# A bench of constant matmuls ahead of the first conditioning product

## The chip, the core and the metric

The kernel runs on one core of a Trainium2 chip. The metric is the device time of one execution in microseconds (us); the lower, the better. Engines are named as in the profile: PE is TensorE's matmul, PEld its weight load, DVE is VectorE, ACT is ScalarE, POOL is GpSimd and SP is SyncE, which here only issues transfers.

## What is computed

One decoder layer is applied to 256 prompt tokens and 32 sample tokens (8 sequences of 4), 288 tokens in all, of width 2048:

```python
def _layer(x, c, conv_prefix, chunk, ...):
    mod = (silu(c) @ w_ada + b_ada).reshape(n, 6, 1, 2048)      # conditioning
    sh_m, sc_m, gt_m, sh_f, sc_f, gt_f = [mod[:, i] for i in range(6)]
    h = _rms(x, g_mix) * (1 + sc_m) + sh_m
    b_gate, c_gate, hc, u, v, ga, gb = split(h @ w_in)          # 2048 -> 9216
    ya = b_gate * short_conv(c_gate * hc)
    yb = gelu(u) * spatial_gate(_rms(gelu(v), g_v))
    merged = sigmoid(ga) * (ya @ w_pa) + sigmoid(gb) * (yb @ w_pb)
    x = x + gt_m * (merged @ w_out)
    h2 = _rms(x, g_ffn) * (1 + sc_f) + sh_f
    gate, up = split(h2 @ w_ffn_in)                             # 2048 -> 2 x 5632
    x = x + gt_f * ((silu(gate) * up) @ w_ffn_out)
```

A last normalisation follows. Returned are the tokens, the new convolution state and the normalised v rows, all in float32.

## The kernel before

Tokens lie along the free dimension and features along the 128 partitions, so a product of 128 output features is a chain of matmuls, each 128x128 weights against 128x288 activations. Every float32 operand is split into a high and a low part in float32r, and one step of a product is three matmuls (`triple`, L221 to L231): high weights with high activations, high weights with low activations, low weights with high activations. These are lines L224, L227 and L229 of the profile, and nearly all of the kernel.

Weights come from memory in blocks of up to 128x2048 into seven rotating buffers named `raw`; ScalarE casts the high part (L448) and VectorE subtracts to get the low part (L454). Activation parts, intermediate results and small tables live in 92 rotating buffers named `s`, of 1,192 bytes per partition each. In the built program a slot begins 32, 96, 160 or 224 bytes past a multiple of 256, and a weight part 96 bytes past one.

The conditioning product `silu(c) @ w_ada` is cut into nine units (a0, a1, aC, aD, aE, a2 to a5) and done by `Ada.run` (L388). The first unit, a0, is the first real work of TensorE. Ahead of it, and in gaps between the first steps, stand matmuls on a bfloat16 tile of ones, `wb`, whose result goes to a PSUM tile `idle` and is read by nobody:

```python
    def warm(n, out=None):
        out = idle if out is None else out
        for _ in range(n):
            PE.matmul(out[:, :T], wb[:, :P], wb, start=True, stop=True)
    ...
    steps = [Do(lambda: warm(24)), a0[0], Do(lambda: warm(5)), a0[1]]
```

TensorE's order is that in which the code is written. The orders of ScalarE, VectorE and SyncE are also the written ones from the first load on, until the head of the kernel is over. A load into a `raw` buffer waits until the tile that had the buffer before has been read for the last time, and all loads are issued from SyncE, one behind the other.

The head goes: load of the two blocks of a0, of the first weights (w0) and the first tile of x, of the two blocks of a1, of the second tile of x, of wK and of the first wA; meanwhile 24 matmuls on ones, a0, the first tile of the activations, the product w0 with it, a1, the second tile, the product wK, and then the stream of weight blocks.

Of the kernel before, what the change touches and what calls it, by code (L numbers as in the profile page):

```python
# [8 lines left out]
F32 = mybir.dt.float32  # L9
F32R = mybir.dt.float32r  # L10
# [4 lines left out]
P = 128  # L15
D = 2048
T = 288
TP = 256
TU = T + 10
# [5 lines left out]
RAW = 7  # L25
# [59 lines left out]
def decoder_kernel(tc, d):  # L85
    nc = tc.nc
    from contextlib import ExitStack

    with ExitStack() as es:
        def pool(name, bufs=1, **kw):  # L90
            return es.enter_context(tc.tile_pool(name=name, bufs=bufs, **kw))

        pc = pool("const")
        pw = pool("wstream")
        pslot = pool("slots", SLOTS)
        ptmp = pool("tmp", 5)
        pps = pool("psum", 4, space=bass.MemoryType.PSUM)
        with tc.manual_schedule(engines={nc.tensor.engine}):
            _body(tc, nc, d, pc, pw, pslot, ptmp, pps)


def _body(tc, nc, d, pc, pw, pslot, ptmp, pps):
    ids = [0]

    def nm(s):
        ids[0] += 1
        return f"{s}_{ids[0]}"

    def const(name, shape, dt=F32):
        return pc.tile(shape, dt, tag=name, name=name)  # L110

    def slot(dt=F32, shape=(P, T)):
        return pslot.tile(list(shape), dt, tag="s", name=nm("s"), padded_shape=[P, TU])
# [4 lines left out]
    def psmain():  # L118
        return pps.tile([P, 512], F32, tag="main", name=nm("pm"), bufs=4)
# [4 lines left out]
    V, A, G, PE, SY = nc.vector, nc.scalar, nc.gpsimd, nc.tensor, nc.sync  # L124
# [227 lines left out]
    class Step:  # L352
        defer = False
        raw = None
# [209 lines left out]
    wb = const("wb", [P, 288], BF16)  # L564
    G.memset(wb, 1.0)
    idle = psmain()
# [475 lines left out]
        tail.close()  # L1042


    rh1 = h1.__getitem__
    def at(main, plan):
        out, n = [], 0
        for s in main:
            out.append(s)
            if isinstance(s, Blk):  # L1050
                n += 1
                out += plan.pop(n, [])
        assert not plan
        return out
# [70 lines left out]
    n = len(steps)  # L1125
    stream = [s for s in steps if not isinstance(s, Do)]
    pos = {id(s): i for i, s in enumerate(stream)}
    order = list(stream)
# [27 lines left out]
    for s in steps:  # L1156
# [11 lines left out]
        i = pos[id(s)]  # L1168
# [124 lines left out]
```

## Time and profile before

| | |
|---|---|
| median of the runs | 1625.04 us (1625.02 to 1625.06, 2 runs) |
| profiled execution, its own time | 1625.02 us |
| its span, first to last instruction | 1623.2 us |
| TensorE matmul, busy | 1613.2 us, 12645 instructions |
| TensorE weight load, busy | 1549.3 us |
| VectorE / ScalarE, busy | 1015.8 / 736.2 us |
| DMA | 357.6 MB, mean 220 GB/s |
| granted TensorE clock | 0.998 |

In a row of groups the columns are line, engine, operation, out<-in by the program's names, shape, number of instructions, then busy time in us and mean ns of one, then the idle time of the engine just before them and what ended it. Matmuls are pipelined: one lasts some 0.29 us from its start to its modelled end while the next has long started, so how fast TensorE works is read from the starts, or from the number of matmuls in a stretch of time.

### The profile page before, as it was taken

The numbers are of one execution on the slowest core, as the hardware profiler recorded it, in microseconds if no ns is written. First come the engines' busy times: TensorE is split into PE (matmuls) and PEld (weight loads), VectorE is DVE, ScalarE is ACT, GpSimd is POOL, SyncE is SP. The second block draws the span as 40 slices with busy tenths as digits, with TensorE's granted clock in tenths as the row PEclk, the third lists the DMA queues.
The fourth block names the chain that finished last, engine by engine and source line by source line (L and its number), as shares of the span: only waits on it lengthen the run. The fifth ranks groups of instructions, "written<-read, shape, count | busy, mean of one in ns | idle before, by whom it ended". The sixth has DMA issues, their size and how long they took to land.

```text
span 1623.2 us, 31599 instructions
## 1 busy us (share of the span) xinstructions
PE 1613.2 (99%) x12645; PEld 1549.3 (95%) x12645; DVE 1015.8 (63%) x2196; ACT 736.2 (45%) x1358; POOL 21.8 (1%) x66
## 2 busy tenths in 40 slices
PE   9999999999999999999999999999999999999997
PEld 8998999999999999999999999999999999999997
DVE  6676788877755567667744555555555555555565
ACT  5533344643444334456633444444444444444454
POOL 0000000000000000011000000000000000000000
PEclk9999999999999999999999999999999999999999
DMA  9887866777877666654576556453464434645341
GB/s 376 324 318 286 313 238 212 273 284 289 298 292 309 261 260 228 241 178 158 185 307 263 207 180 209 156 173 110 164 229 157 168 121 161 225 157 172 110 161 59
DMA packets 59140, 357.60 MB, mean 220 GB/s; under 512 B 6736, under 2 KB 9840, under 8 KB 28272
## 3 DMA queue, kind: packets, MB, share of 16 engines
q1 hardware_dynamic: 58704, 355.45, 60.0%
q8 instruction: 99, 1.62, 0.4%
q14 instruction: 49, 0.40, 0.1%
q10 hardware_dynamic: 288, 0.13, 0.0%
HBM read 352.46 MB, written 3.09 MB: 219 GB/s over the span
## 4 chain that ended last, share of the span: by engine, by line
PE 98%; DMA 1%; DVE 0%; DVEq 0%; ACT 0%; issue 0%; ACTq 0%
PE pm L224 31%; PE pm L227 31%; PE pm L229 30%; PE ada L388 5%; DMA raw<-in_wK 1%; DMA raw<-in_w 0%; DVE st L1023 0%; DMA ct<-in_c 0%; PE px L227 0%; PE px L818 0%; PE px L224 0%; PE px L229 0%; PE px L859 0%; PE px L198 0%; PE px L860 0%; PE px L861 0%
## 5 line engine op out<-in xcount | busy, mean ns | idle before, releaser
L224 PE MATMUL pm<-s,hi 128*128 128x288 f32 (+1 forms) x3750 | 1108.9, 296 | 0.0
L227 PE MATMUL pm<-s,hi 128*128 128x288 f32 (+1 forms) x3750 | 1105.0, 295 | 0.0
L229 PE MATMUL pm<-s,lo 128*128 128x288 f32 (+1 forms) x3738 | 1101.3, 295 | 0.0
L448 ACT CAST hi<-raw 128x512 fp32r<-128x512 f32 (+1 forms) x963 | 587.4, 612 | 812.0 <-PE pm L227 776.7
L454 DVE TENSOR_TENSOR lo<-raw,hi 128x512 fp32r<-128x512 f32 (+1 forms) x849 | 577.2, 681 | 439.2 <-ACT hi L448 426.8
L224 PEld LDWEIGHTS pm<-s,hi 128*128 128x128 f32 x3750 | 705.1, 188 | 15.2 <-issue 13.3
L227 PEld LDWEIGHTS pm<-s,hi 128*128 128x128 f32 x3750 | 704.7, 188 | 0.0
L229 PEld LDWEIGHTS pm<-s,lo 128*128 128x128 f32 x3738 | 702.7, 188 | 0.0
L243 DVE TENSOR_TENSOR lo<-raw,hi 128x512 fp32r<-128x512 f32 x111 | 74.7, 676 | 29.6 <-ACT hi L448 28.9
L388 PE MATMUL ada<-raw,cs 128*32 128x512 f32 (+2 forms) x1152 | 88.3, 452 | 0.0
L388 PEld LDWEIGHTS ada<-raw,cs 128*32 128x32 f32 x1152 | 30.9, 110 | 44.7 <-issue 42.0
L766 DVE TENSOR_TENSOR s<-pm,s 128x288 f32<-128x288 f32 x72 | 32.9, 457 | 19.8 <-PE pm L229 19.8
L298 DVE TENSOR_TENSOR s<-t,s 128x288 fp32r<-128x288 f32 (+1 forms) x76 | 34.6, 459 | 6.4 <-ACT s L296 6.4
L296 ACT CAST s<-t 128x288 fp32r<-128x288 f32 (+1 forms) x76 | 32.5, 433 | 12.9 <-DVE t L798 12.4
L338 DVE SCALAR_TENSOR_TENSOR x<-pm,mod,x 128x256 f32<-128x256 f32 x79 | 37.5, 475 | 0.0
L944 DVE SCALAR_TENSOR_TENSOR t<-t,pm 128x288 f32<-128x288 f32 x42 | 19.1, 454 | 20.6 <-PE pm L229 20.6
L758 DVE TENSOR_TENSOR s<-pm,s 128x288 f32<-128x288 f32 x48 | 21.8, 454 | 10.4 <-PE pm L229 9.5
L337 DVE TENSOR_TENSOR t<-pm,mod 128x32 f32<-128x32 f32 x79 | 15.2, 192 | 18.5 <-PE pm L229 18.5
L743 DVE SCALAR_TENSOR_TENSOR s<-pm,s 128x256 f32<-128x256 f32 x48 | 23.1, 480 | 4.1 <-PE pm L229 4.1
L749 DVE TENSOR_TENSOR s<-s,rb 128x288 f32<-128x288 f32 x48 | 21.5, 449 | 0.0
L172 ACT ACTIVATE t<-x 128x288 f32<-128x288 f32 x29 | 12.9, 445 | 17.4 <-DVE x L341 17.4
L177 DVE TENSOR_TENSOR acc<-acc,t 128x288 f32<-128x288 f32 x33 | 15.0, 456 | 8.2 <-ACT t L172 8.2
(158 smaller groups left out, 479.7 us busy)
## 6 DMA issues: line engine op xcount, KB each, us to landing
raw<-in_fi SPq DMA_DIRECT2D x84, 1024.0 KB, 4.9
raw<-in_a SPq DMA_DIRECT2D x64, 1024.0 KB, 8.8
raw<-in_f SPq DMA_DIRECT2D x64, 704.0 KB, 4.0
raw<-in_wD SPq DMA_DIRECT2D x34, 1024.0 KB, 5.7
raw<-in_aE SPq DMA_DIRECT2D x16, 1024.0 KB, 10.3
raw<-in_wo SPq DMA_DIRECT2D x16, 1024.0 KB, 6.4
raw<-in_wC SPq DMA_DIRECT2D x19, 768.0 KB, 5.7
raw<-in_pa SPq DMA_DIRECT2D x8, 1024.0 KB, 5.9
```

What stands on the lines that cost most here:

```text
L224: PE.matmul(out, wh, ah, start=first, stop=False)
L227: end_ = PE.matmul(out, wh, al, start=False, stop=turn and last)
L229: end_ = PE.matmul(out, wl, ah, start=False, stop=last)
L243: lows.pop(0)[1]()
L296: A.copy(hi, a)
L298: V.tensor_tensor(lo, a, hi.bitcast(F32), ALU.subtract)
L338: V.scalar_tensor_tensor(x[:, m, :TP], ps[:, :TP], mod[:, gt0 + m, 0:1], x[:, m, :TP], ALU.mult, ALU.add)
L388: PE.matmul(acc[32 * j : 32 * j + 32, :w], cs[:, kt, :], self.raw[:, o : o + w], start=kt == 0, stop=kt == 15, tile_position=(0, 32 * j), ...
L448: A.copy(hi, self.raw[:, s * 128 : e * 128])
L454: sub()
L743: V.scalar_tensor_tensor(t[:, :TP], ps[:, :TP], t[:, T : T + 1], t[:, :TP], ALU.add, ALU.add)
L766: V.tensor_tensor(a, ps[:, :T], a, ALU.add)
```

## The change

A function `bench` is added and called once, before the steps of the program are put together, so its instructions stand ahead of all other work in each engine's written order. It takes four `raw` buffers and 64 `s` buffers, fills one with the constant 0.75, copies that into three float32r tiles (r0, r1, r2) and into the 64 slots, and has TensorE multiply them into `idle`: first 48 matmuls on `wb`; then weights from r0 and activations from r2, both shifted by 1 to 4 elements, the activations in 64 places; then pairs of weights and activations in the main product's order of three at chosen places; then the same order with activations from slots and weights shifted by 0 to 15 elements. No result is read. The outputs and the rest of the program are the same, apart from the buffers that it gets.

```diff
+    def bench():
+        import random
+
+        f = pw.tile([P, 2048], F32, tag="raw", name=nm("bench"), bufs=RAW)
+        V.memset(f, 0.75)
+        rs = []
+        for i in range(3):
+            r = pw.tile([P, 2048], F32R, tag="raw", name=nm("benchr"), bufs=RAW)
+            A.copy(r, f) if i else V.tensor_copy(r, f)
+            rs.append(r)
+        r0, r1, r2 = rs
+        ms = []
+        for i in range(64):
+            m = slot(F32R, (P, TU))
+            (A.copy if i % 2 else V.tensor_copy)(m, f[:, :TU])
+            ms.append(m)
+
+        def mm(s, m):
+            PE.matmul(idle[:, :T], s, m, start=True, stop=True)
+
+        def w(r, k, s=0):
+            return r[:, P * (k % 12) + s : P * (k % 12) + s + P]
+
+        def mv(r, o):
+            return r[:, o : o + T]
+
+        for i in range(48):
+            mm(wb[:, :P], wb)
+        for s in (1, 2, 3, 4):
+            for o in range(64):
+                for i in range(14):
+                    mm(w(r0, i, s), mv(r2, o + s))
+        rng = random.Random(1)
+        for a in [12 + 16 * i for i in range(16)] + [144, 48, 240, 0]:
+            for b in rng.sample(range(64), 16):
+                for i in range(6):
+                    mm(w(r0, i), mv(r2, a // 4))
+                    mm(w(r0, i), mv(r2, 512 + a // 4))
+                    mm(w(r1, i, b), mv(r2, a // 4))
+        order = "212030111323010323020333020010212333202030202131"
+
+        def mixed(sh, sl, n):
+            for i in range(16):
+                h, l = (ms[(4 * i + 2 * j + int(order[3 * i + j]) % n) % 64 // 4 * 4 + int(order[3 * i + j]) % n * (4 // n)][:, :T] for j in (0, 1))
+                mm(w(r0, i, sh), h)
+                mm(w(r0, i, sh), l)
+                mm(w(r1, i, sl), h)
+
+        for s in range(16):
+            mixed(s, s, 2)
+        for sh in range(16):
+            for sl in range(16):
+                mixed(sh, sl, 4)
+
+    bench()
```

TensorE's queue at the start of the program, before. The first matmuls are those on ones, the next the first conditioning block (`ada` is its PSUM tile, `raw` its weights, `cs` the conditioning vectors):

```order
L1278 UNCONDITIONAL_BRANCH [waits barrier_Pool_Activation_PE_DVE_SP_release]
L571 LDWEIGHTS wb [waits Pool_49]
L571 MATMUL pm_96<-wb 128x288
...
L388 MATMUL ada_164<-raw_99,cs 32x64 [waits DMAHW1_49,DVE_49]
L388 MATMUL ada_164<-raw_99,cs 32x64 x15
```

The same place in the changed program. `benchr_99`, `benchr_101` and `benchr_103` are r0, r1 and r2, a name with `s` is one of the 64 slots, `pm_96` is `idle`:

```order
L1333 UNCONDITIONAL_BRANCH [waits barrier_Pool_Activation_PE_DVE_SP_release]
L1063 LDWEIGHTS wb [waits Pool_49]
L1063 MATMUL pm_96<-wb 128x288
...
L1063 MATMUL pm_96<-benchr_103,benchr_99 128x288 [waits DVE_49,Activation_49]
L1063 MATMUL pm_96<-benchr_103,benchr_99 128x288 x3585
L1063 MATMUL pm_96<-benchr_103,benchr_101 128x288
...
L1063 MATMUL pm_96<-s_105,benchr_99 128x288 [waits DVE_49]
...
L571 LDWEIGHTS wb
L571 MATMUL pm_96<-wb 128x288
...
L388 MATMUL ada_22748<-raw_22683,cs 32x64 [waits DMAHW2_49]
```

The whole bench has come between the program's start and the first matmuls on ones of before; it waits for the constants at its first float32r matmul and at the slots, and for nothing else.

SyncE's queue from the third conditioning block on, before (a `DMAHW` semaphore counts earlier transfers):

```order
L370 DMA raw_111<-in_a 128x1024 [waits DMAHW3_49]
L370 DMA raw_111<-in_a 128x1024 [waits DMAHW4_49]
L370 DMA raw_114<-in_a 128x1024 [waits DMAHW5_49]
L370 DMA raw_114<-in_a 128x1024 [waits DMAHW6_49]
L146 DMA x<-in_x 128x288 [waits DMAHW7_49]
L432 DMA raw_118<-in_wK 128x768 [waits DMAHW0_49]
L432 DMA raw_120<-in_wA 128x1024 [waits DMAHW1_49]
```

And in the changed program, where the third block gets the buffer of the constant fill, the fourth that of r0, wK that of r1 and wA that of r2:

```order
L370 DMA raw_22695<-in_a 128x1024 [waits DMAHW3_49,DVE_49,Activation_49]
L370 DMA raw_22695<-in_a 128x1024 [waits DMAHW4_49]
L370 DMA raw_22698<-in_a 128x1024 [waits DMAHW5_49,PE_49]
L370 DMA raw_22698<-in_a 128x1024 [waits DMAHW6_49]
L146 DMA x<-in_x 128x288 [waits DMAHW7_49]
L432 DMA raw_22702<-in_wK 128x768 [waits DMAHW0_49,PE_49]
L432 DMA raw_22704<-in_wA 128x1024 [waits DMAHW1_49,PE_49]
```

The order of the loads is the same; three of them now wait for TensorE, the third conditioning block for the copies on VectorE and ScalarE.

## The prediction

> **What bounds the kernel now.** I read the page first: its span, the busy shares, the granted clock and the chain that ended last.
>
> ```profile
> span 1623.2 us, 31599 instructions
> PE 1613.2 (99%) x12645; PEld 1549.3 (95%) x12645; DVE 1015.8 (63%) x2196; ACT 736.2 (45%) x1358; POOL 21.8 (1%) x66
> PEclk9999999999999999999999999999999999999999
> PE 98%; DMA 1%; DVE 0%; DVEq 0%; ACT 0%; issue 0%; ACTq 0%
> ```
>
> TensorE is busy for 99% of the span, the clock is granted throughout, and 98% of the chain that set the end is TensorE's own work. There is no idle time in which added TensorE work could disappear: what is put into its queue moves the end by what it takes. So the whole question is how fast TensorE goes through it.
>
> The duration of a matmul does not tell that, since matmuls overlap. The pace, from one start to the next, does. I took it from the stage table, in three stretches that hold little beside the main product (columns: the stretch, its length, then busy time and number of instructions of each engine, granted clock, DMA share, GB/s).
>
> ```profile
> core 0: us, PE busy (x) PEld busy (x) DVE busy (x) ACT busy (x) POOL busy (x), PEclk, DMA share, GB/s
> 900.00:1200.00 300.00, 300.00 (x2271) 300.00 (x2270) 166.03 (x328) 128.45 (x224) 0.00 (x0) 1.00 0.51 171
> 1200.00:1500.00 300.00, 300.00 (x2273) 300.00 (x2272) 163.18 (x300) 131.44 (x229) 0.00 (x0) 1.00 0.49 167
> 1500.00:1600.00 100.00, 100.00 (x758) 100.00 (x757) 60.25 (x129) 53.21 (x99) 0.00 (x0) 1.00 0.34 116
> ```
>
> 300 us over 2273 matmuls is 0.1320 us; over 2271 it is 0.1321 us, and 100 over 758 is 0.1319 us. The pace of the 128x288 product with float32r operands is therefore 0.132 us, and it stays there while the DMA share falls from 0.51 to 0.34, so transfers into the memory that TensorE reads do not set it. A look at single instructions shows the same steps of 0.13 and 0.14 us with no idle time between:
>
> ```profile
> 1250.25 0.29 PE L224 MATMUL pm<-s,hi 128*128 128x288 f32 x1
> 1250.39 0.29 PE L227 MATMUL pm<-s,hi 128*128 128x288 f32 x1
> 1250.52 0.30 PE L229 MATMUL pm<-s,lo 128*128 128x288 f32 x1
> 1250.65 0.29 PE L224 MATMUL pm<-s,hi 128*128 128x288 f32 x1
> ```
>
> Last I read the start of the program in order of time, because the change stands there.
>
> ```profile
> 1.12 5.24 PE L571 MATMUL pm<-wb 128*128 128x288 bf16 x24 [1.12 <-POOL wb L565]
> 4.83 0.32 ACT L155 ACTIVATE ctt<-ct 128x144 f32<-128x144 f32 x1 [1.90 <-DMA ct<-in_c]
> 6.29 1.10 PE L388 MATMUL ada<-raw,cs 128*32 128x64 f32 x64
> 7.32 0.79 PE L571 MATMUL pm<-wb 128*128 128x288 bf16 x5
> 9.43 0.62 ACT L448 CAST hi<-raw 128x512 fp32r<-128x512 f32 x1 [4.27 <-DMA raw<-in_w]
> 10.05 1.15 PE L571 MATMUL pm<-wb 128*128 128x288 bf16 x8
> 11.36 0.82 PE L501 MATMUL pm<-s,hi 128*128 128x298 f32 x4 [0.15 <-ACT s L677]
> 12.02 0.71 PE L503 MATMUL pm<-s,lo 128*128 128x298 f32 x4
> 17.87 1.21 PE L388 MATMUL ada<-raw,cs 128*32 128x64 f32 x64
> ```
>
> The first conditioning product is the row at 6.29. Ahead of it stand 24 matmuls on constants in bfloat16. A row of several merged matmuls lasts from the first start to the last end, so two rows of one kind give the pace: (1.15 - 0.79) / 3 = 0.12 us for bfloat16 later on. The 24 went slower: the end of the last lies about 0.79 - 4 x 0.12 = 0.31 us behind its start, so (5.24 - 0.31) / 23 = 0.214 us each.
>
> **The change part by part.** It removes and reorders nothing. It adds 22,448 matmuls, all 128x288, to the head of TensorE's queue: 48 on the bfloat16 constant, then 4 x 64 x 14 = 3584, then 20 x 16 x 6 x 3 = 5760, then 16 x 16 x 3 = 768 and 256 x 16 x 3 = 12288 on float32r constants. The last four make 22,400.
>
> *The 48 in bfloat16.* TensorE still starts at 1.12. The first 24 take 5.24 us as before, the other 24 take 24 x 0.12 = 2.9 us: they end at 9.24.
>
> *Making the constants.* One VectorE fill, one VectorE and two ScalarE copies of 2048 columns stand before the first float32r matmul. ScalarE reaches its two copies behind the activation that ends at 4.83 + 0.32 = 5.15. The cast of 512 columns took 0.62 us, so four of them bound one copy from above at 2.48 us, and both end by 10.1 at the latest. If the cost of a copy is partly fixed, they end before 9.24. I take 9.24, with 0 to 0.9 us of wait. The 64 small copies that follow are first read after 3584 + 5760 matmuls, over a millisecond later, which hides them.
>
> *The 22,400 in float32r.* Same shape, types and order as the main product, each with its own weights, no accumulation, one output bank. At 0.132 us they take 2956.8 us. What the trace does not show is a start address of weights or activations off the main product's places, so this price needs ends. Below, it is the pace of the bfloat16 constants, 0.12 us: 2688 us. Above, it is a pace at which a weight load no longer hides behind the matmul before it. The weight loads have this row:
>
> ```profile
> L224 PEld LDWEIGHTS pm<-s,hi 128*128 128x128 f32 x3750 | 705.1, 188 | 15.2 <-issue 13.3
> L224 PE MATMUL pm<-s,hi 128*128 128x288 f32 (+1 forms) x3750 | 1108.9, 296 | 0.0
> ```
>
> One load lasts 188 ns, so that end is 22,400 x 0.188 = 4211 us. I take 0.132, the row that is nearest: it has the same operation, shape and types, and in it the activation tiles already start at four different places in 256 bytes against one place of the weights, with no difference between stages. That no result is accumulated changes little: the four first matmuls at 11.36, which do not accumulate, start 12.02 - 11.36 = 0.66 us ahead of the next group, 0.165 us each with a slow first, and the accumulating four at 12.02 go at (0.71 - 0.30) / 3 = 0.137 us for 298 columns.
>
> The Trainium skill, "TensorE: Matmul & The Clock Gate", section "Back-to-back issue gap", gives the warm gap as N / 2.4 + 2.5 ns, which is 122.5 ns at 288 columns. The bfloat16 rows agree with it (0.12 us) and the float32r stages don't (0.132 us); by it the 22,400 would be estimated at 2744 us.
>
> *What stands behind them.* Everything from the row at 1.12 on now starts when the last of them has started. From there the old program has 1623.2 - 1.12 = 1622.1 us. Its 24 constants now run at the later pace: 1.15 + 16 x 0.12 = 3.07 instead of 5.24 us, 2.2 us less. The head's transfers are the other part. Of the seven load buffers the change occupies four; the first two conditioning blocks, the first weights and the third conditioning block land long before TensorE asks for them. The fourth conditioning block waits on SyncE until TensorE has read the constants for the last time, and behind it on that queue wait the second tile of x, the next weights (wK) and all later loads. Before, the critical chain had this load:
>
> ```profile
> 10.53 9.19 DMA raw<-in_wK
> ```
>
> 9.19 us is the longest landing of the head. The fourth block is asked for at 17.87, which is 17.87 - 1.12 - 2.2 = 14.6 us behind the release, so it is covered by about 5 us, and fewer transfers compete. Were that cover gone, the excess, a few us, would be paid once. wK is issued right behind it, earlier against its use than the 10.53 - 1.12 - 2.2 = 7.2 us of before. So the queue costs nothing, and TensorE's gaps in the head can at most close:
>
> ```profile
> 10.00:20.00 10.00, 9.85 (x189) 8.67 (x180) 6.64 (x21) 4.26 (x12) 0.10 (x1) 1.00 1.04 405
> 20.00:30.00 10.00, 9.66 (x69) 9.34 (x68) 7.60 (x18) 8.82 (x19) 0.00 (x0) 1.00 1.02 406
> ```
>
> That is 0.15 + 0.34 us; I count 0.2. The rest takes 1622.1 - 2.4 = 1619.7 us. The tiles of the main product move to other buffers, which by the three stages (0.1319 to 0.1321) is worth 12,000 x 0.0002 = 2.4 us either way.
>
> *The sum.* 9.24 + 2956.8 + 1619.7 = 4585.7 us of span. The profiled execution took 1625.02 us for a span of 1623.2, 1.8 more, and the median of the two runs is 1625.04, the same. The forecast is 4585.7 + 1.8 = 4587.5, rounded to 4588 us.
>
> **The rivals.** *The added product goes at the bfloat16 pace.* The main product may lose 0.012 us per matmul to a conflict between reading weights and reading activations that depends on their places; places that avoid it would give 0.12 us and 9.24 + 2688 + 1619.7 + 1.8 = 4319 us. For it speaks that single steps of 0.13 and 0.14 alternate. Against it: the change goes through nearly all places, so it would have to help at most of them. A time under 4460, a mean pace under 0.1263, gets 0.07. The gap formula named above is this case.
>
> *Odd places make weight loads or reads slow.* At the upper end it gives 9.24 + 4211 + 1619.7 + 1.8 = 5842 us, and if half the matmuls are hit (5842 + 4588) / 2 = 5215 us. No row shows a start that is not a multiple of 32 bytes, so nothing speaks against it directly; but the load has room, since a pace of 0.132 is kept with loads of 188 ns that overlap. Over 4720, a mean pace over 0.138, gets 0.09. Constants that leave the clock at its early pace (0.214 us, some 6430 us) are within it at 0.01; the bfloat16 constants did reach 0.12.
>
> *Not slower: matmuls whose result nobody reads do not run.* Then 48 + 22,400 would fall away and the time would be 1625 us or less by the 2.2 us. It decides once fewer than (32.5 - 5.7) / 0.132 = 203 of the 22,400 run, 32.5 us being 2% (about what a measurement of this kernel can tell from no change) and 5.7 us the net cost of the 48. Against it: the constants of L571 are read by nobody either, and the trace has them. The built order has every added matmul. 0.015.
>
> **How the numbers follow.** The likeliest case, a mean pace within 0.1263 to 0.138, has 0.825 and gives 4588 us. The range is its own, 4460 to 4720: the lower end lies halfway from 0.132 to 0.12, the upper just past the 0.137 us that the wider 298-column product shows at 12.02 (22,400 x 0.137 + 1630.7 = 4700). It leaves out 0.07 below, 0.09 above and 0.015 far below. All cases but the last are slower by over 2%: slower 0.985, same 0.01, faster 0.005.
>
> **What would show it.** Right: a group of 22,400 matmuls ahead of the conditioning product, no idle time in it, a stage table with 2270 or so matmuls in each 300 us, the granted clock at 1.00, and the row that was at 6.29 at about 2969 us, with the end about 1617 us behind it. Also right: DMA nearly still from about 25 us to 2966. Wrong: stages inside the added product whose paces differ by more than 5%, which would make the place of an operand a price of its own; idle time before its first float32r matmul beyond 1 us; a wait on the fourth conditioning block or on wK behind it.

## The result, and the profile after

The changed kernel takes 4598.29 us (median of 2 runs, 4598.27 to 4598.31) against 1625.04 us, a ratio of 2.8296 with a 95% interval of 2.8175 to 2.8418. The forecast was 4588 us with a range of 4460 to 4720.

The page of the changed kernel, its top and two of its groups:

```profile
span 4596.5 us, 76567 instructions
PE 4586.0 (100%) x35093; PEld 4521.1 (98%) x35093; DVE 1026.7 (22%) x2230; ACT 750.3 (16%) x1392; POOL 21.3 (0%) x66
PEclk9999999999999999999999999999999999999999
PE 100%; DVE 0%; ACT 0%; DMA 0%; issue 0%; DVEq 0%
L1063 PE MATMUL pm<-s,benchr 128*128 128x288 f32 x13056 | 1732.4, 295 | 0.0
L1063 PE MATMUL pm<-benchr,benchr 128*128 128x288 f32 x9344 | 1234.3, 294 | 0.2 <-ACT benchr L1053 0.2
```

All 9344 + 13056 = 22,400 matmuls ran, with 0.2 us of idle time ahead of them and none between. TensorE is busy throughout and the clock is granted. The stage table of TensorE, in stretches of the bench's four float32r parts (500 to 800 and 1000 to 1230 lie in the second, 1240 to 1345 is nearly all of the third, the last two lie in the fourth):

```profile
core 0: us, PE busy (x), PEclk, DMA share, GB/s
9.30:300.00 290.70, 290.70 (x2183) 1.00 0.02 7
500.00:800.00 300.00, 300.00 (x2287) 1.00 0.00 1
1000.00:1230.00 230.00, 230.00 (x1751) 1.00 0.00 1
1240.00:1345.00 105.00, 105.00 (x793) 1.00 0.04 12
2000.00:2300.00 300.00, 300.00 (x2264) 1.00 0.00 1
2600.00:2900.00 300.00, 300.00 (x2264) 1.00 0.00 1
```

The paces are 290.7 / 2183 = 0.1332 us, 0.1312, 0.1314, 0.1324, 0.1325 and 0.1325. They are within some 1.5% of each other and of the main product's 0.1320 before. A stretch also counts the two or three matmuls that reach into it from before its start, so paces read in this way are 0.1 to 0.3% low. The two ends of the bench, and what follows it, in order of time:

```profile
1.12 7.55 PE L1063 MATMUL pm<-wb 128*128 128x288 bf16 x48 [1.12 <-POOL wb L565]
8.86 21.40 PE L1063 MATMUL pm<-benchr,benchr 128*128 128x288 f32 x159 [0.20 <-ACT benchr L1053]
2975.27 3.11 PE L571 MATMUL pm<-wb 128*128 128x288 bf16 x24
2978.31 1.10 PE L388 MATMUL ada<-raw,cs 128*32 128x64 f32 x64
2983.38 0.68 PE L501 MATMUL pm<-s,hi 128*128 128x298 f32 x3 [0.15 <-ACT s L677]
2984.69 0.30 PE L501 MATMUL pm<-s,hi 128*128 128x298 f32 x1 [0.63 <-issue]
```

The float32r part lasts from 8.86 to 2975.27, 2966.4 us, and the rest of the program from there to 4596.5, 1621.2 us.

### The profile page after: what moved, and what is told of

Read it like the earlier page. It is cut to its first block, busy times and chain, and to the rows that moved or that the text cites. A ratio compares the mean times of both kernels' runs of the same rounds, so it can differ in the third digit from the quotient of the medians.

```text
span 4596.5 us, 76567 instructions
## 1 busy us (share of the span) xinstructions
PE 4586.0 (100%) x35093; PEld 4521.1 (98%) x35093; DVE 1026.7 (22%) x2230; ACT 750.3 (16%) x1392; POOL 21.3 (0%) x66
## 4 chain that ended last, share of the span: by engine, by line
PE 100%; DVE 0%; ACT 0%; DMA 0%; issue 0%; DVEq 0%
PE pm L1063 65%; PE pm L224 11%; PE pm L227 11%; PE pm L229 11%; PE ada L388 2%; PE pm L571 0%; DVE st L1023 0%; DMA ct<-in_c 0%; ACT benchr L1053 0%; PE px L227 0%; PE px L224 0%; PE px L818 0%; PE px L229 0%; PE px L859 0%; PE px L198 0%; PE px L860 0%
## 5 line engine op out<-in xcount | busy, mean ns | idle before, releaser
L1063 PE MATMUL pm<-s,benchr 128*128 128x288 f32 x13056 | 1732.4, 295 | 0.0
L1063 PEld LDWEIGHTS pm<-s,benchr 128*128 128x128 f32 x13056 | 1732.3, 188 | 0.0
L1063 PEld LDWEIGHTS pm<-benchr,benchr 128*128 128x128 f32 x9344 | 1234.1, 188 | 0.5 <-ACT benchr L1053 0.5
L1063 PE MATMUL pm<-benchr,benchr 128*128 128x288 f32 x9344 | 1234.3, 294 | 0.2 <-ACT benchr L1053 0.2
L338 DVE SCALAR_TENSOR_TENSOR x<-pm,mod,x 128x256 f32<-128x256 f32 x79 | 37.5, 474 | 0.0
```

Source lines behind the costliest of these rows:

```text
L338: V.scalar_tensor_tensor(x[:, m, :TP], ps[:, :TP], mod[:, gt0 + m, 0:1], x[:, m, :TP], ALU.mult, ALU.add)
L1063: PE.matmul(idle[:, :T], s, m, start=True, stop=True)
```

## The experiments

**Half of the work.** The last pair of nested loops of the bench go.

```diff
-        for sh in range(16):
-            for sl in range(16):
-                mixed(sh, sl, 4)
```

> The last loop of the bench, 12,288 of the 22,400 float32r matmuls, is left out; all else stands. If the added time is a sum of equal pieces (theory: 0.1326 us each, the pace that the trace of the changed kernel shows for that stretch), 12,288 x 0.1326 = 1629 us go and 2969 us are left, within 5. If the pace drifts with the length of the added work (rival: the clock or the memory gives way late in a long run, so the last part is dearer or cheaper than the first), the rest differs from 2969 by 1% or more, 30 us.

Measured: 2970.25 us, one run. The added time shrank by 4598.3 - 2970.3 = 1628.0 us for 12,288 matmuls, 0.1325 us each. That is the pace of this part in the stage table, so the added time is a sum of the parts' own times; a drift with the length of the work would have shown 30 us or more.

**Only the 48 in bfloat16.** All float32r work, the constants and their buffers are left out; the lines are shown against the changed kernel.

```diff
-        f = pw.tile([P, 2048], F32, tag="raw", name=nm("bench"), bufs=RAW)
...
         for i in range(48):
             mm(wb[:, :P], wb)
-        for s in (1, 2, 3, 4):
...
```

> Only the 48 bfloat16 matmuls are added, with none of the constants, so no buffer is held and nothing waits. Theory by the prediction's terms: 48 take 7.6 to 8.1 us from 1.12 on, the 24 behind them go 2.1 us faster than before, 1.7 us of the head's waits can close or open: 1625.0 + 7.7 - 2.1 = 1630.6 us, 1629 to 1632. Rival that work on constants whose result nobody reads is free, or hidden behind the head's transfers: 1625 or less. Rival that the saving behind the bench is not there: 1632.7.

Measured: 1628.62 us, one run, beside 1625.09 for the kernel before on the same chip: 3.5 us more where 5.5 were expected, and just under the expected 1629 to 1632. Unread matmuls are not free. Its head in order of time:

```profile
1.12 7.49 PE L1049 MATMUL pm<-wb 128*128 128x288 bf16 x48 [1.12 <-POOL wb L565]
8.45 3.10 PE L571 MATMUL pm<-wb 128*128 128x288 bf16 x24
11.48 1.10 PE L388 MATMUL ada<-raw,cs 128*32 128x64 f32 x64
16.55 0.68 PE L501 MATMUL pm<-s,hi 128*128 128x298 f32 x3 [0.16 <-ACT s L677]
17.80 0.30 PE L501 MATMUL pm<-s,hi 128*128 128x298 f32 x1 [0.57 <-issue]
```

The 24 matmuls take 3.10 us instead of 5.24, the saving that the prediction counted (3.07). The conditioning product starts 11.48 - 6.29 = 5.2 us later than before; the span is only 1626.8 - 1623.2 = 3.6 us longer, so 1.6 us were won back behind it, which was not expected. One new gap stands there too: 0.57 us between the third and the fourth matmul of the first tile's product, which the profile lays on no other engine. The changed kernel has the same gap with 0.63 us.

No run was made to find the cause of the gap, so it stays open, but the traces point to the program's code. The page has a queue for instructions (packets, MB, share), first before, then changed:

```profile
q8 instruction: 99, 1.62, 0.4%
q8 instruction: 274, 4.49, 0.4%
```

The 175 packets more are 16 KB each, one for every 128 of the 22,400 matmuls. In all eight runs with added matmuls their number is 48 more than a multiple of 128, so the late matmul stands at the same place within a packet; all eight have the gap, of 0.48 to 1.62 us, and in all eight the late matmul starts 2.3 to 2.5 us after such a transfer has started. The three kernels without added matmuls have no gap there.

**Data instead of constants.** Rows of the aE weights are loaded in place of the constant 0.75; the copies into r0, r1, r2 and the slots, cut here, read them.

```diff
-        V.memset(f, 0.75)
+        fs = [f] + [pw.tile([P, 2048], F32, tag="raw", name=nm("bench"), bufs=RAW) for _ in range(2)]
+        for i, t in enumerate(fs):
+            SY.dma_start(t, d["aE"][i])
...
```

> The same bench, with rows of the aE weights in place of the constant 0.75 in r0, r1, r2 and the 64 slots; three loads of 1 MB are added at the start. Theory (the pace does not hang on the values): 4598 us, up to 5 more for the loads. Rival (constants are cheaper than data, for the clock or otherwise): the pace of the bench rises by 2% or more, 4660 us or above.

Measured: 4606.03 us, one run, 7.7 us more than the changed kernel and 3 above what was expected, far from 4660. In the stage table the pace is the same from 2000 to 2300 (0.1325); the other row is the start:

```profile
core 0: us, PE busy (x), PEclk, DMA share, GB/s
13.09:18.00 4.91, 4.91 (x20) 0.50 0.00 0
2000.00:2300.00 300.00, 300.00 (x2264) 1.00 0.00 1
```

The surplus stands at the start:

```profile
13.09 27.21 PE L1065 MATMUL pm<-benchr,benchr 128*128 128x288 f32 x185 [4.15 <-ACT benchr L1055]
```

The first float32r matmul starts 4.2 us later, because it waits for the loads (13.09 against 8.86). Then 185 matmuls go at (27.21 - 0.29) / 184 = 0.1463 us, against (21.40 - 0.29) / 158 = 0.1336 in the changed kernel: 184 x 0.0127 = 2.3 us more. The row above shows where: behind the idle time the granted clock is 0.50 until 18.00, and 20 matmuls fill 4.91 us, 0.245 us each. The gap before the fourth matmul on the first tile is 0.9 us longer (1.56 us against 0.63). Together this is some 7.5 of the 7.7 us. The values have no price in the pace.

**What the 0.132 us is made of.** Nine loops of 1024 matmuls take the place of the bench; each differs from the first in one size, type or operand.

```diff
+        for i in range(1024):
+            PE.matmul(idle[:, :T], w(r0, i), r2[:, :T], start=True, stop=True)
+        for i in range(1024):
+            PE.matmul(idle[:64, :T], w(r0, i, 64), r2[:, :T], start=True, stop=True)
...
+            PE.matmul(idle, w(r0, i), r2[:, :512], start=True, stop=True)
...
+            PE.matmul(idle[:, :T], w(wide, i), wide[:, :T], start=True, stop=True)
+        for i in range(1024):
+            PE.matmul(idle[:, :T], w(r0, i), r2[:, :1].to_broadcast([P, T]), start=True, stop=True)
...
```

> Nine loops of 1024 matmuls in place of the bench, each on a line of its own, to see what makes the float32r pace 0.132 us where the bfloat16 constants have 0.122 (0.010 us more). In this order: 128 weight columns and 288 activations; 64 weight columns; 32 weight columns; 512, 256 and 128 activations; bfloat16 with a new weight each time; all activations from one column; all weights from one column. A, the reads of weights and activations get in each other's way while a load runs: 0.132, 0.127, 0.124, 0.226, 0.118, then near 0.122 for bfloat16 and for one column of activations. B, a fixed cost of a float32r matmul: 0.132, 0.132, 0.132, 0.226, 0.118, 0.064, bfloat16 0.122, 0.132, 0.132. C, a float32r column is slower: 0.132, 0.132, 0.132, 0.235, 0.117, 0.059. D, the load of 128 weight columns sets the pace: 0.132, then 0.122 at 64 and 32 columns, 0.216 at 512, and 0.132 still at 256 and at 128 activations. The whole is near 2850 us by B.

Measured: 2890.76 us, one run, where B had some 2850. The groups by shape (busy us, then mean ns of one; the pace is busy less one duration, over 1023):

```profile
L1065 PE MATMUL pm<-benchr,benchr 128*128 128x288 f32 x1024 | 135.1, 294 | 0.0
L1067 PE MATMUL pm<-benchr,benchr 128*64 128x288 f32 x1024 | 133.3, 292 | 0.0
L1069 PE MATMUL pm<-benchr,benchr 128*32 128x288 f32 x1024 | 134.4, 294 | 0.0
L1071 PE MATMUL pm<-benchr,benchr 128*128 128x512 f32 x1024 | 232.3, 389 | 0.0
L1073 PE MATMUL pm<-benchr,benchr 128*128 128x256 f32 x1024 | 123.0, 283 | 0.0
L1075 PE MATMUL pm<-benchr,benchr 128*128 128x128 f32 x1024 | 114.5, 274 | 0.0
L1077 PE MATMUL pm<-benchb 128*128 128x288 bf16 x1024 | 125.6, 286 | 0.0
L1079 PE MATMUL pm<-benchr,benchr 128*128 128x288 f32 x1024 | 128.6, 287 | 0.0
L1081 PE MATMUL pm<-benchr,benchr 128*128 128x288 f32 x1024 | 135.3, 294 | 0.0
```

The first has (135.1 - 0.294) / 1023 = 0.1318 us. 64 weight columns give 0.1300 and 32 give 0.1311, where A wanted 0.127 and 0.124 and D 0.122: the weight load is not what makes the pace at 288 activations. All weights from one column change nothing (0.1320). 512 activations take 0.2267 and 256 take 0.1200, so a column costs 0.1067 / 256 = 0.000417 us and 13.3 ns are left over per matmul (11.7 ns at 288 by the same price of a column); C, which wanted 0.235, is out. B fits these to within 2 ns. It fails at two places. At 128 activations the pace is 0.1117 where B has 0.064; with so few columns something else binds, perhaps the weight load; that was not tried. This also makes up the 40 us by which the whole is above B: 1024 x 0.0477 = 49 us, of which the loop with one column of activations gives 7 back. With all activations from that one column the pace is 0.1254, so 6 of the 9 ns above bfloat16 (0.1225) go with how the activations are read; what makes the other 3 stays open.

**One place for all activations.** The bench with every float32r activation tile 28 bytes past a multiple of 32, and in another kernel 4 bytes.

```diff
         def mv(r, o):
+            o = o // 8 * 8 + 7
             return r[:, o : o + T]
...
-                h, l = (...[:, :T] for j in (0, 1))
+                h, l = (...[:, 7 : 7 + T] for j in (0, 1))
...
```

At 4 bytes the two edits read `// 8 * 8 + 1` and `1 : 1 + T`.

> The bench with every float32r activation tile starting 28 bytes past a multiple of 32; weights, shapes and counts as in the changed kernel. In the trace of the changed kernel the first loop has mean paces of 130.6 ns at such starts, 132.6 at 0, 132.1 at 12 and 16, 134 at 8 and 24, 135.1 at 4 and 20, with 448 matmuls each. Theory that the place prices the matmul by a per cent or two, and fast and slow places average out in the bench: 22,400 x (130.6 - 132.4) = -40 us, 4558. Rival that the place has no price and the pattern comes from the loop: 4598.

> The same with every activation tile 4 bytes past a multiple of 32. Theory that the place has a price: 22,400 x (135.1 - 132.4) = +60 us, 4659. Rival without a price: 4598.

Measured: 4564.33 us at 28 bytes and 4665.58 us at 4 bytes, one run each, where 4558 and 4659 were expected and 4598 without a price. The stage tables, first of 28 bytes, then of 4:

```profile
100.00:400.00 300.00, 300.00 (x2302) 1.00 0.00 1
2000.00:2300.00 300.00, 300.00 (x2293) 1.00 0.00 1
```

```profile
100.00:400.00 300.00, 300.00 (x2222) 1.00 0.00 1
2000.00:2300.00 300.00, 300.00 (x2218) 1.00 0.00 1
```

The paces are 0.1303 to 0.1308 and 0.1350 to 0.1353 us. So the place has a price of 3.5% between these two. In the bench as it was the mean is 2966.4 / 22,400 = 0.1324, near the main product's 0.1320. This is not only an average over places: the slots start at multiples of 32 bytes, as in the main product, and 13,056 of the 22,400 matmuls read slots. Most of the second part stands at 12 and 28 bytes, and only the first 3584 go through all eight places evenly. The starts at 8, 20 and 24 bytes, which the expectation above lists as slow too, had no run of their own.

**The same places in the main product.** The kernel before, without a bench; its 288-column slots start 7 elements (28 bytes) or 1 element (4 bytes) later in the same buffers.

```diff
-        return pslot.tile(list(shape), dt, tag="s", name=nm("s"), padded_shape=[P, TU])
+        t = pslot.tile([P, TU], dt, tag="s", name=nm("s"))
+        o = 7 if shape[1] <= T else 0
+        return t[:, o : o + shape[1]]
```

> The kernel before, without any bench, whose 288-column slots start 28 bytes later inside the same buffers, so that the activations of 10,878 of its matmuls start 28 bytes past a multiple of 32 instead of at 0. Theory that the place has the price seen in the bench, 130.6 against 132.6 ns: 10,878 x 0.0020 = 22 us less, 1603, and 1608 if the gain is that against the main product's own 132.1. Rival that the main product's pace is set otherwise (its slots stand differently to the weights, and other engines use them too): 1625; if VectorE or ScalarE lose on odd starts, above it.

> The same with slots that start 4 bytes later. Theory that the place has the price seen in the bench, 135.1 against 132.1 to 132.6 ns: 27 to 33 us more, 1652 to 1658. Rival without a price: 1625.

Measured: 1619.97 us at 28 bytes, a ratio of 0.9968 (95% interval 0.9957 to 0.9980) to the kernel before; 1662.55 us at 4 bytes, 1.0230 (1.0213 to 1.0247). One stage of each, first 28 bytes, then 4:

```profile
900.00:1200.00 300.00, 300.00 (x2279) 1.00 0.50 171
```

```profile
900.00:1200.00 300.00, 300.00 (x2221) 1.00 0.49 172
```

From 900 to 1200 the paces are 300 / 2279 = 0.1316 and 300 / 2221 = 0.1351 us, against 0.1321 before. The price at 4 bytes is there in full and more (37.6 us, 27 to 33 expected). The gain at 28 bytes is a quarter of the 22 us expected: 5.0 us. Both are all in TensorE's pace: by the starts of the 10,878 matmuls in the traces, the mean step is 3.45 ns longer at 4 bytes (37.5 us in all) and 0.48 ns shorter at 28 (5.2 us). The version at 28 bytes is still the fastest of the kernel here.

**Per matmul or per column, and the distance of two tiles.** Thirteen more loops of 1024.

```diff
+        for i in range(1024):
+            PE.matmul(idle, w(r0, i), r2[:, 0 : 512], start=True, stop=True)
+        for i in range(1024):
+            PE.matmul(idle, w(r0, i), r2[:, 7 : 519], start=True, stop=True)
+        for i in range(1024):
+            PE.matmul(idle, w(r0, i), r2[:, 1 : 513], start=True, stop=True)
...
+        for i in range(1024):
+            PE.matmul(idle[:, :T], w(r0, i), (r1, r2)[i % 2][:, 7 + 32 * (i % 2) : 7 + 32 * (i % 2) + T], start=True, stop=True)
...
```

> Thirteen loops of 1024 matmuls in place of the bench, each on its own line. First three: 512 activations that start 0, 28 and 4 bytes past a multiple of 32. If the place of the activations is a price per matmul: 226.7 (measured before), 225, 229.5 ns. If it is a price per column: 226.7, 224, 232. Then 288 activations at 28 and at 4: 131 and 135.5 by the two benches with one place. Then activations at 0 and weights 4 bytes off: 131.8 if only the activations' place counts, 134 or more if any odd place does. Then bfloat16 at 28 and at 4 bytes: 122.5 both if the price belongs to float32r alone, 121 and 125 if to the place. Last five: activations in turn from two tiles, both at 28 bytes, 8192 bytes apart and then 128, 512, 1024 and 1920 bytes more: 131 in all five if only the start within 32 bytes counts; one of them at 134 or above if the distance of two tiles that follow each other also counts, which the kernel before with its slots at 28 bytes points to (131.7 instead of 131.0, with single steps of 141).

Measured: 3663.66 us, one run. The groups (512 activations at 0, 28 and 4 bytes; 288 at 28 and 4; weights at 4; bfloat16 at 28 and 4; then two tiles in turn, 0, 128, 512, 1024 and 1920 bytes off):

```profile
L1065 PE MATMUL pm<-benchr,benchr 128*128 128x512 f32 x1024 | 232.4, 389 | 0.0
L1067 PE MATMUL pm<-benchr,benchr 128*128 128x512 f32 x1024 | 232.3, 387 | 0.0
L1069 PE MATMUL pm<-benchr,benchr 128*128 128x512 f32 x1024 | 242.5, 399 | 0.0
L1071 PE MATMUL pm<-benchr,benchr 128*128 128x288 f32 x1024 | 133.3, 291 | 0.0
L1073 PE MATMUL pm<-benchr,benchr 128*128 128x288 f32 x1024 | 139.0, 300 | 0.0
L1075 PE MATMUL pm<-benchr,benchr 128*128 128x288 f32 x1024 | 135.0, 294 | 0.0
L1077 PE MATMUL pm<-benchb 128*128 128x288 bf16 x1024 | 126.0, 285 | 0.0
L1079 PE MATMUL pm<-benchb 128*128 128x288 bf16 x1024 | 125.6, 285 | 0.0
L1081 PE MATMUL pm<-benchr,benchr 128*128 128x288 f32 x1024 | 133.4, 291 | 0.0
L1083 PE MATMUL pm<-benchr,benchr 128*128 128x288 f32 x1024 | 135.0, 293 | 0.0
L1085 PE MATMUL pm<-benchr,benchr 128*128 128x288 f32 x1024 | 133.3, 291 | 0.0
L1087 PE MATMUL pm<-benchr,benchr 128*128 128x288 f32 x1024 | 133.3, 291 | 0.0
L1089 PE MATMUL pm<-benchr,benchr 128*128 128x288 f32 x1024 | 135.0, 293 | 0.0
```

At 4 bytes 512 activations cost 10.0 ns more than at 28 (0.2367 against 0.2267), and 288 cost 5.6 ns more (0.1356 against 0.1300): the same 0.02 ns per column, so that price grows with the columns and is not one per matmul. The advantage of 28 over 0 (0.1300 against 0.1318) is gone at 512, so against a start at 0 the price of 4 bytes is 3.8 ns at 288 columns and 9.9 at 512, and neither expectation was met in full. Weights at 4 bytes cost nothing (0.1317), and bfloat16 shows no price of the place (0.1229 and 0.1225). Two tiles in turn that lie 128 or 1920 bytes off a multiple of 8192 go at 0.1317, at 0, 512 and 1024 bytes at 0.1300 or 0.1301: how the next tile lies to this one counts as well, 1.7 ns here. The expected 134 or above was not seen. 1.7 ns is also about what the main product misses at 28 bytes, but this does not show that the distance of its slots is the cause. Against it speaks the last part of the bench at 28 bytes, which goes through slots in four relative places in turn and has 0.1308. Why the main product gains only a quarter stays open.

## Why the prediction was right

**The bound.** TensorE was read as busy for 99% with no room, so that added work would come on top. It did: 4596.5 us of span, 4586.0 of them busy, and 55% of the work left out took 55% of the added time with it.

**The main term.** 22,400 x 0.132 = 2956.8 us was predicted, 2966.4 us measured: 0.3% too little, the largest miss of the sum. Some 4 us of the 9.6 lie in the reading: by their starts the matmuls of the main product between 900 and 1500 are 0.1322 us apart on average, where the count in a stretch gave 0.1320, and 22,400 x 0.0002 = 4.5 us. The step that carried it, that the nearest row is the main product's own pace and not either end (0.12 or 0.188), held. Its reason held only in part. The prediction argued that four places of the activations already occur without a difference; all four are multiples of 32 bytes, and the place within 32 bytes does have a price, from 0.130 to 0.136 us. That the forecast came so close is in part luck: 13,056 of the added matmuls happen to stand at such multiples, and the fast and slow places of the others, which the prediction did not tell apart, average out near them. With all tiles at 4 bytes it would have missed by 78 us and still lain in the range.

**The other terms.** The float32r work starts at 8.86 instead of 9.24. The 24 constants behind it take 3.11 us where 3.07 were predicted. The rest was 1621.2 us where 1619.7 were predicted: the 0.63 us gap in the first tile's product is new, and the remainder is within what this stretch varies (1621.1 to 1623.2 us in the half bench, with data and in the two with one place). Together -0.4, 9.6 and 1.5 make up the 10.8 us by which the span was longer, up to rounding.

**The queue of loads.** No wait of TensorE on the fourth conditioning block or on wK shows, as forecast, but the fourth block was not covered in the way that was forecast. Its two halves and wK were issued here:

```profile
1243.20 0.80 SPq L370 DMA_DIRECT2D raw<-in_a  x2
2975.32 0.33 SPq L432 DMA_DIRECT2D raw<-in_wK  x1
```

In the built program the fourth block has the buffer of r2, wK that of r0 and wA that of r1, not r0, r1 and r2 as listed with the change. r2 is read for the last time when the second part ends at 1243, so the fourth block lay in memory 1.7 ms before its use, and a cover of 5 us was never at stake. wK was the first load to wait for the last constant. It landed in 3.1 us instead of 9.2 and was first read at 2988.54, over 13 us after its issue. (9.2 us was not the longest landing of the head either: the first half of wA took 9.9.)

**The rivals.** The pace of the bfloat16 constants was not reached at any place that was tried; the reason given for it, a conflict between reading weights and activations, is contradicted by the loops with fewer weight columns. Odd places can be slower, but by 2.9% at the worst that was tried with 288 columns (0.1356 against 0.1318) and not by 42%. Constants that leave the clock at its early pace are ruled out by the stage table, where no pace is above 0.1332 us. Unread matmuls do run. The formula of the Trainium skill, "TensorE: Matmul & The Clock Gate", section "Back-to-back issue gap", agrees with bfloat16 at 288 columns (122.5 ns by it and 0.1225 us measured) and is 9 to 11 ns short for float32r at 256, 288 and 512 columns.

## What to carry to other kernels

When an engine has no idle time, the cost of added work is a count times its pace, and the pace is read from the number of instructions in a stretch of time, not from the mean duration of one. In this kernel a start of the streamed float32r operand 4 bytes past a multiple of 32 cost 2.3%, so where such a start can be chosen, keep off it; the start of the weights did not matter. A load waits for the last reading of the buffer that it gets, so look up which buffer that is before counting its cover. A pace that was only seen at some places should be called known for these places alone.

## What was not expected of the hardware

The place of the float32r activations within 32 bytes moved the pace between 0.130 and 0.136 us at 288 columns, and the same shift in bfloat16 or of the weights makes no more than 0.4 ns. After 4.2 us in which TensorE waited for loads, the profile has a granted clock of 0.50 for the next 4.9 us, and 2.3 us were lost there.
